# Attention over 512 queries per block of keys, with probabilities of four query tiles weighted together, in a hybrid attention and retention block on one Trainium2 core

## The chip, the cores and the metric

The program runs on one core of a Trainium2 chip. A core has a matrix engine, TensorE (PE in the profile; PEld is its weight load, which runs ahead of the matmuls), a VectorE (DVE), a ScalarE (ACT), a GpSimd (POOL) and a SyncE (SP), which here only issues transfers. Each engine has its own queue of instructions in program order, and they meet through semaphores. The metric is the device time of one execution in microseconds; the median of three runs is given.

## The reference

One layer over 2048 tokens of width 1024: an RMS norm, one input projection to ten pieces (7168 columns), two branches, a gated merge, an output projection and a last RMS norm. The branch that matters here is attention: 8 heads of width 64, in which a chunk of 64 frames attends to itself and the eight chunks before it, with a clipped relative bias.

```python
qc = qb.reshape(n_chunks, CHUNK, H, d)
k_band = jnp.concatenate([kp[i:i + n_chunks] for i in range(N_LEFT_CHUNKS + 1)], axis=1)
v_band = jnp.concatenate([vp[i:i + n_chunks] for i in range(N_LEFT_CHUNKS + 1)], axis=1)
s = jnp.einsum('nqhd,nkhd->nhqk', qc, k_band).astype(jnp.float32) * scale + bias[None]
s = jnp.where(valid[:, None, None, :], s, NEG_INF)
w = jax.nn.softmax(s, axis=-1).astype(vb.dtype)
o = jnp.einsum('nhqk,nkhd->nqhd', w, v_band)
```

The other branch is retention (8 heads, keys of 64, values of 128, in chunks), and each branch has its own output projection and gate.

## The kernel before

The large projections are **dense** work: a Strassen scheme over operands that are split into a high and a low float32r part, three matmuls of 128x512 per weight pair. It is one long generator, cut into steps; one step is three such matmuls on TensorE (some 0.7 us) with whatever their preparation and evacuation need elsewhere. Attention and retention run in two sequences, for the first 1024 tokens and then for the last, and between their own instructions they call `fill(n)`, which takes n steps of the dense generator. `later(n, fn)` puts work on a list that is issued n steps later, so the order of the instructions on every engine is written out by the step counter: TensorE, SyncE and (in these stages) all the other engines keep that program order (`Ordered`). In the attention stages the dense work is the gate projection (names ps_g, wh_g, wl_g, raw_g, t_g, u_g, c_g).

Queries come in blocks of 512 (b = 0..3), and a block in four tiles of 128 (t = 0..3). Before, a **unit** is a head, a block and a half (un): two query tiles, a = 0 and 1. For a unit `soft` (twice) multiplies the tile's queries by its 640 keys into the PSUM tile wide (four matmuls, 384 and 256 columns; less on block 0, which has no block before it). One step later VectorE adds the bias and takes the row minimum (`least`, the custom instruction pr<-wide,bt), one more step later ScalarE takes the exponentials with their sum (`exps`), and after four steps VectorE inverts the sum and GpSimd scales the row (`normed`, pr<-pr,rsum). Then `weighted` turns the probabilities (pr) with transposes into a PSUM tile tp, in three groups of two key tiles each, one group per step. ScalarE writes the high part (pth), one step later VectorE the low part (ptl<-tp,pth), and three steps after the transposes (PV_LAG) TensorE multiplies the values (va) by both parts into po. Each product is 128x256: key tile j times the two query tiles of the unit. A pair (key tile, query tile) that lies outside the band is a block of zeros in pth and ptl, set by a VectorE MEMSET. In the first and last group of a unit one of four blocks is such zeros. `out_` evacuates po after the second half.

A unit takes six steps (line 1585 on: soft, `fill(2 * ATT_FILL)`, soft, `fill(ATT_FILL)`, three groups with a fill each; one or two groups on block 0). 18 steps of dense work stand between the first loads of a stage and its first scores, 12 after its last group. Tiles of pools rotate: four pr tiles of 128x640 (PR_BUFS), and twelve 128x512 tiles of the pool E (E_ATT) for queries, values, pth, ptl, gates and results. ps_acc has four PSUM banks, for dense accumulators and tp both. Loads (qa queries, ka keys, va values, ua gates) are issued on SyncE's queue.

Of the kernel before, what the change touches and what calls it, by code (L numbers as in the profile page):

```python
# [21 lines left out]
P = 128  # L22
# [50 lines left out]
def hybrid_kernel(  # L73
# [30 lines left out]
    def r32(ap):  # L104
        return ap.bitcast(F32)
# [1306 lines left out]
    def attention(s, sbp, ps_wide):  # L1412
# [1 line left out]
        wide = ps_wide.tile([P, 1536], F32, tag="wide", name="wide")  # L1414
        po = ps_wide.tile([P, 512], F32, tag="po", name="po")
        kts, vts, qts, bts, uts, oas, prs = {}, {}, {}, {}, {}, {}, {}
        units = [(h, b, un) for h in range(HEADS) for b in (2 * s, 2 * s + 1) for un in range(2)]

        def load_k(h, b):
            kts[h, b] = sbp.tile([P, 2 * B], F32R, tag="kt", bufs=2, name=f"ka_{h}_{b}")  # L1420
# [52 lines left out]
            later(1, close)  # L1473
            later(0, far)

        def soft(h, b, un, a):

            t = 2 * un + a
# [18 lines left out]
            pr = sbp.tile([P, WIN], F32, tag="pr", bufs=PR_BUFS, name=f"pr_{nm}")  # L1497
            mn = small.tile([P, 1], F32, tag="mn", name=f"mn_{nm}")
            rsum = small.tile([P, 1], F32, tag="rsum", name=f"rsum_{nm}")
            bt = bts[h]  # L1500

            def least():
                dve.tensor_tensor_reduce(
                    pr[:, 0:w], sp, bt[:, WIN - w:WIN], 1.0, 3.0e38, ALU.add, ALU.min, mn,
                )

            def exps():
                act.activation(pr[:, 0:w], pr[:, 0:w], AF.Exp, bias=mn, scale=-1.0, accum_out=rsum)

            def normed():  # L1510
                dve.reciprocal(rsum, rsum)
# [5 lines left out]
            return pr  # L1517

        def weighted(h, b, un, pr2):

            nk = 6 if b > 0 else 2 * un + 2
            lo = [0, 1] if b > 0 else [0, 0]
            hi = [nk - 1, nk]
            o = po[:, un * 256:(un + 1) * 256]
            for gr in range(nk // 2):
                js = [2 * gr + 1, 2 * gr] if gr in (0, nk // 2 - 1) else [2 * gr, 2 * gr + 1]
                tp = ACC(f"tp_{h}_{b}_{un}_{gr}")
                ok, none, parts = [], [], []
                for n, j in enumerate(js):
                    for a in range(2):  # L1530
                        c = (2 * n + a) * P
                        if lo[a] <= j < hi[a]:
                            pe.transpose(
                                tp[:, c:c + P], pr2[a][:, (j - lo[a]) * P:(j - lo[a] + 1) * P], ident
                            )
                            ok.append(c)
                        else:
                            none.append(c)
                c0, c1 = ok[0], ok[-1] + P
                assert c1 - c0 == len(ok) * P  # L1540

                def part(which, gr=gr, tp=tp, none=none, parts=parts, c0=c0, c1=c1):
                    t = E(f"pt{which}_{h}_{b}_{un}_{gr}", F32R)
                    parts.append(t)
                    for c in none:
                        dve.memset(r32(t[:, c:c + P]), 0.0)
                    if which == "h":
                        act.copy(t[:, c0:c1], tp[:, c0:c1])
                    else:
                        dve.tensor_tensor(t[:, c0:c1], tp[:, c0:c1], r32(parts[0][:, c0:c1]), ALU.subtract)  # L1550

                def product(gr=gr, js=js, parts=parts):
                    for n, j in enumerate(js):
                        k = 2 * un + j if b > 0 else j + 4
                        v4 = vts[h, b - 1 + k // 4][:, k % 4, :]
                        for i, t in enumerate(parts):
                            pe.matmul(
                                o, v4, t[:, 256 * n:256 * n + 256],
                                start=(gr == 0 and n == 0 and i == 0),
                                stop=(gr == nk // 2 - 1 and n == 1 and i == 1),  # L1560
                            )
                    if gr == nk // 2 - 1:
                        later(1, out_)

                part("h")
                later(1, lambda part=part: part("l"))
                later(PV_LAG, product)
                yield

            def out_():  # L1570
                if un == 0:
                    return
# [4 lines left out]
                put(6, oascr[h // 2][b][64 * (h % 2):64 * (h % 2) + 64], oa)  # L1577

        load_bias(0)
        load_k(0, 2 * s)  # L1580
        load_q(0, 2 * s, 0)
        fill(12)
        turn_bias(0)
        fill(6)
        for m in range(len(units) + 1):
            if m < len(units):
                h, b, un = units[m]
                if m + 1 < len(units):
                    h2, b2, un2 = units[m + 1]
                    load_q(h2, b2, un2)  # L1590
                if un == 0 and m + 2 < len(units):
                    load_k(*units[m + 2][0:2])
                if un:
                    load_u(h, b)
                if (b, un) == (2 * s, 0) and h + 1 < HEADS:
                    load_bias(h + 1)
                if (b, un) == (2 * s + 1, 0) and h + 1 < HEADS:
                    turn_bias(h + 1)
                prs[m] = [soft(h, b, un, 0)]
                fill(2 * ATT_FILL)  # L1600
                prs[m].append(soft(h, b, un, 1))
                fill(ATT_FILL)
            if m:
                for _ in weighted(*units[m - 1], prs.pop(m - 1)):
                    fill(ATT_FILL)
            if m < len(units) and un == 0:
                later(PV_LAG - 1, lambda h=h, b=b: load_vs(h, b))
        fill(PV_LAG + 9)


    def retention(s, ps_ret):
# [427 lines left out]
```

## Time and profile before

| what | us |
|---|---|
| median of three runs (lowest, highest) | 1945.7 (1945.29, 1947.35) |
| the profiled execution: its time, its span | 1943.98, 1942.2 |
| TensorE matmul busy | 1887.3 (97%) |
| VectorE, ScalarE, GpSimd busy | 1355.7, 930.9, 898.4 |
| attention's score matmuls (wide), first and last start | 348.0 to 1321.7 |
| products with the values (po<-pth and po<-ptl), 336 each | 92.5 and 88.3 busy |
| VectorE MEMSET of pth and ptl, 112 each | 18.5 and 18.5 busy |

Attention stands at 348 to 562 us and at 1077 to 1335 us of the span, a retention stage behind each. Busy time of TensorE is a union of instructions whose ends are modelled, about 0.28 us for a 128x256 matmul; how fast they follow each other is read from the starts in the timeline. A row of a group reads: busy time, mean of one in ns, idle time before, and what ended it.

### The profile page before, as it was taken

The page shows a single profiled execution, that of the slowest core. Times are in us where ns is not written, and L with a number is a line of the kernel's source. Part 1 is how long each engine was busy: PE and PEld are TensorE (multiplying, and loading weights), DVE is VectorE, ACT ScalarE, POOL GpSimd, SP SyncE. Part 2 cuts the span into 40 slices and gives each one's busy share as a digit, 9 for nine tenths or more (in the row PEclk, how much of TensorE's full clock was granted, in tenths as well). Part 3 has the DMA queues.
Part 4 walks back from the last instruction along what each step waited for, and adds up shares of the span by engine and source line. Part 5 has one row for each costly group of instructions (what it writes and reads, how often), then busy time and mean ns, then how long its engine had stood idle before and what let it go on. Part 6 is the DMA issues. An engine that isn't in the chain of part 4 may idle for free. (4 is left out here: it accounts for less than half of the span.)

```text
span 1942.2 us, 31900 instructions
## 1 busy us (share of the span) xinstructions
PE 1887.3 (97%) x10437; PEld 1617.8 (83%) x10437; DVE 1355.7 (70%) x2521; ACT 930.9 (48%) x1931; POOL 898.4 (46%) x742
## 2 busy tenths in 40 slices
PE   7999999999999999999999999999999999999998
PEld 6899879888888887899879888888888878887886
DVE  6969788677756558879788677765555654547665
ACT  7544553666654545343333666664455321223554
POOL 0313525545545566323415544544564114557775
PEclk9999999999999999999999999999999999999999
DMA  6586876565559978575666555555998999977673
GB/s 195 169 279 194 255 263 217 182 192 177 175 156 277 270 239 298 186 257 187 196 222 209 158 166 174 160 155 160 272 274 269 313 357 330 320 261 237 208 240 127
DMA packets 325750, 435.93 MB, mean 224 GB/s; under 512 B 30073, under 2 KB 191377, under 8 KB 325585
## 3 DMA queue, kind: packets, MB, share of 16 engines
q1 hardware_dynamic: 260096, 368.35, 59.3%
q10 hardware_dynamic: 65488, 65.55, 11.2%
q8 instruction: 83, 1.36, 0.3%
q14 instruction: 83, 0.67, 0.1%
HBM read 288.14 MB, written 145.64 MB: 223 GB/s over the span
## 5 line engine op out<-in xcount | busy, mean ns | idle before, releaser
L142 POOL TENSOR_SCALAR pr<-pr,rsum 128x640 f32<-128x640 f32 (+4 forms) x128 | 96.5, 754 | 212.2 <-DVE ptl L142 99.8
L142 PE MATMUL ps_g_z<-r,wh_g 128*128 128x512 f32 x448 | 144.0, 403 | 1.4 <-DVE c_g L142 1.4
L142 PE MATMUL ps_g_x<-r,wh_g 128*128 128x512 f32 x448 | 143.2, 401 | 1.0 <-ACT u_g L142 0.8
L142 DVE CUSTOM_DVE_ANT_0 pr<-wide,bt 128x640 f32<-128x640 f32 (+4 forms) x128 | 94.3, 737 | 61.8 <-PE wide L142 49.7
L142 ACT ACTIVATE pr<-pr,mn 128x640 f32<-128x640 f32 (+4 forms) x128 | 98.0, 766 | 81.9 <-DVE mn L142 81.9
L142 DVE TENSOR_TENSOR ptl<-tp,pth 128x384 fp32r<-128x384 f32 x168 | 96.1, 573 | 41.2 <-ACT pth L142 37.9
L142 ACT CAST pth<-tp 128x384 fp32r<-128x384 f32 x168 | 84.5, 515 | 68.0 <-PE tp L142 64.8
L142 POOL TENSOR_TENSOR l_vr<-vrt,h_vr 128x512 fp32r<-128x512 f32 x32 | 46.8, 1463 | 121.0 <-DMA qrs<-l_q 81.3
L142 POOL TENSOR_TENSOR sl<-sm,sh 128x384 fp32r<-128x384 f32 x64 | 68.9, 1077 | 70.5 <-ACT sh L142 48.2
L142 PEld LDWEIGHTS tp<-ident,pr 128*128 128x128 f32 x560 | 71.1, 140 | 27.4 <-POOL pr L142 2.9
L142 DVE TENSOR_TENSOR sm<-sr,dm 128x384 f32<-128x384 f32 x64 | 35.6, 556 | 82.8 <-DMA dm<-in_dmask_dram 26.3
L142 POOL TENSOR_TENSOR wl_g<-t_g,wh_g 128x512 fp32r<-128x512 f32 x56 | 75.0, 1340 | 39.5 <-ACT wh_g L142 39.2
L142 PE MATMUL po<-pth,va 128*128 128x256 f32 x336 | 92.5, 296 | 0.0
L142 PE MATMUL tp<-ident,pr 128*128 128x128 f32 x560 | 89.3, 272 | 2.9 <-POOL pr L142 1.7
L142 ACT CAST wh_p<-raw_p 128x512 fp32r<-128x512 f32 x99 | 61.3, 621 | 61.7 <-PE ps_p_y L142 23.3
L142 PE MATMUL wide<-ka,qa 128*128 128x384 f32 (+1 forms) x448 | 88.3, 313 | 2.3 <-DVE mn L142 2.1
L142 PEld LDWEIGHTS wide<-ka,qa 128*128 128x128 f32 x448 | 74.5, 188 | 18.9 <-DVE mn L142 9.0
L142 PE MATMUL po<-ptl,va 128*128 128x256 f32 x336 | 88.3, 284 | 1.4
L142 PE MATMUL ps_g_z<-r,wl_g 128*128 128x512 f32 x224 | 88.3, 394 | 0.0
L142 PE MATMUL ps_g_x<-r,wl_g 128*128 128x512 f32 x224 | 88.1, 393 | 0.0
L142 DVE TENSOR_TENSOR wl_p<-raw_p,wh_p 128x512 fp32r<-128x512 f32 x99 | 82.4, 836 | 5.4 <-ACT wh_p L142 5.4
L142 POOL TENSOR_TENSOR t_g<-raw_g,t_g 128x512 f32<-128x512 f32 x56 | 73.7, 1316 | 24.6 <-DVE wl_g L142 10.6
(933 smaller groups left out, 6263.0 us busy)
## 6 DMA issues: line engine op xcount, KB each, us to landing
raw_g<-in_w_in_dram ACTq DMA_DIRECT2D x56, 512.0 KB, 4.3
raw_p<-in_w_in_dram ACTq DMA_DIRECT2D x38, 512.0 KB, 5.8
qa<-qas SPq DMA_DIRECT2D x128, 128.0 KB, 3.1
qr<-qrs SPq DMA_DIRECT2D x128, 128.0 KB, 4.6
vr<-vrs SPq DMA_DIRECT2D x64, 256.0 KB, 5.9
ka<-kas SPq DMA_DIRECT2D x56, 256.0 KB, 3.4
va<-vas SPq DMA_DIRECT2D x40, 256.0 KB, 3.3
kds<-kdt_k SPq DMA_DIRECT2D x32, 256.0 KB, 3.3
```

Source lines behind the costliest of these rows:

```text
L142: return tc.keep_in_program_order(op(*a, **k))
```

## The change

A unit is now a head and a block: all four query tiles, `weighted` with six groups of key tiles (0,1), 2, 3, 4, 5, (7,6), of which block 0 has the last three. A product takes key tile j with only those query tiles that see it: 1, 2, 3, 4, 4, 3, 2, 1 tiles for j = 0 to 7, that is 128 to 512 columns; the transposes put just these side by side, and the memsets of zero blocks are gone. On block 0 the four query tiles' probabilities (128, 256, 384 and 512 columns) share two pr tiles. There are five pr tiles for four, and eleven E tiles for twelve. A unit's steps are numbered: `plan` says at which of 12 steps (9 on block 0) each group of this unit and each `soft` of the next unit is issued, `slot` issues them, and one fill stands behind every slot. The first group's product comes four steps after its transposes, the others three. Ahead of a stage's first scores stand 12 + 2 steps and the slots of an empty unit, behind its last product 6. The number of dense steps in a stage is the same.

```diff
-E_ATT = 12
+E_ATT = 11
-PR_BUFS = 4
+PR_BUFS = 5
...
-        units = [(h, b, un) for h in range(HEADS) for b in (2 * s, 2 * s + 1) for un in range(2)]
+        units = [(h, b) for h in range(HEADS) for b in (2 * s, 2 * s + 1)]
...
-        def weighted(h, b, un, pr2):
-
-            nk = 6 if b > 0 else 2 * un + 2
...
-                    for c in none:
-                        dve.memset(r32(t[:, c:c + P]), 0.0)
...
-                            pe.matmul(
-                                o, v4, t[:, 256 * n:256 * n + 256],
...
+                pair, at = (t, 0) if b > 0 else ((0, 0), (1, 0), (1, 2 * P), (0, P))[t]
+                if (h, b, pair) not in wholes:
+                    wholes[h, b, pair] = sbp.tile([P, WIN], F32, tag="pr", bufs=PR_BUFS, name=f"pr_{nm}")
+                prs[h, b, t] = wholes[h, b, pair][:, at:at + w]
...
+        def weighted(h, b, gr):
+
+            k0 = 0 if b > 0 else 4
+            js = ((0, 1), (2,), (3,), (4,), (5,), (7, 6))[gr]
+            tp = ACC(f"tp_{h}_{b}_{gr}")
+            c, cut, parts = 0, [], []
+            for j in js:
+                ts = range(max(0, j - 4), min(4, j + 1))
+                cut.append((j, c, ts))
+                for t in ts:
+                    at = (j - max(t, k0)) * P
+                    pe.transpose(tp[:, c:c + P], prs[h, b, t][:, at:at + P], ident)
+                    c += P
...
+            def product():
+                for j, at, ts in cut:
+                    n = len(ts) * P
+                    v4 = vts[h, b - 1 + j // 4][:, j % 4, :]
+                    for i, p in enumerate(parts):
+                        pe.matmul(
+                            po[:, ts[0] * P:ts[0] * P + n], v4, p[:, at:at + n],
...
+            part("h")
+            later(1, lambda: part("l"))
+            later(PV_LAG + (gr == 0), product)
+
+        def plan(b):
+
+            if b == 0:
+                return 9, {2: 3, 4: 4, 6: 5}, {1: 0, 3: 1, 5: 2, 7: 3}
+            return 12, {0: 0, 2: 1, 4: 2, 6: 3, 8: 4, 10: 5},                 {2: 0, 6: 1, 8: 2, 10: 3} if s else {2: 0, 4: 3, 6: 1, 8: 2}
...
         load_bias(0)
-        load_k(0, 2 * s)
-        load_q(0, 2 * s, 0)
+        load_k(*units[0])
+        load_q(*units[0], 0)
         fill(12)
         turn_bias(0)
-        fill(6)
...
-        fill(PV_LAG + 9)
+        fill(2)
+        for m in range(-1, len(units)):
+            length, *plans = plan(units[m][1] if m >= 0 else 2 * s + 1)
+            for n in range(length):
+                slot(m, n, *plans)
+                if n == length - 2 and m + 2 < len(units):
+                    load_q(*units[m + 2], 0)
+                if n == length - 1 and m + 1 < len(units):
+                    load_vs(*units[m + 1])
+                fill(ATT_FILL if m >= 0 or n > 1 else 0)
+        fill(PV_LAG + 3)
```

Three places show how the instructions moved. In the names the head's number is left out, so pth_2_0 is block 2, group 0 (before: block 2, half 0, group 0 is pth_2_0_0). First TensorE in the second attention stage, block 2: the products of a first group before,

```order
L142 MATMUL po<-pth_2_0_0_13109,va_1_13082 128x256
L142 MATMUL po<-ptl_2_0_0_13116,va_1_13082 128x256
L142 MATMUL ps_g_1_z<-r_86,wh_g_1_4_12987 128x512
L142 MATMUL ps_g_1_z<-r_87,wh_g_1_4_12987 128x512
L142 MATMUL ps_g_1_z<-r_86,wl_g_1_4_12988 128x512
L142 MATMUL wide<-ka_3_13024,qa_3_0_13063 128x384
L142 MATMUL wide<-ka_3_13024,qa_3_0_13063 128x256
```

(the second of the two key tiles; the first has the same two rows just ahead) and now:

```order
L142 MATMUL po<-pth_2_0_13294,va_1_13275 128x128
L142 MATMUL po<-ptl_2_0_13306,va_1_13275 128x128
L142 MATMUL po<-pth_2_0_13294,va_1_13275 128x256
L142 MATMUL po<-ptl_2_0_13306,va_1_13275 128x256
L142 MATMUL ps_g_2_v<-r_90,wh_g_2_2_13109 128x512
L142 MATMUL ps_g_2_v<-r_91,wh_g_2_2_13109 128x512
L142 MATMUL ps_g_2_v<-r_90,wl_g_2_2_13110 128x512
L142 MATMUL tp_2_2_13352<-ident,pr_2_0_13139 128x128
L142 MATMUL tp_2_2_13352<-ident,pr_2_1_13204 128x128
L142 MATMUL tp_2_2_13352<-ident,pr_2_2_13233 128x128
L142 MATMUL tp_2_2_13352<-ident,pr_2_3_13270 128x128
```

The first key tile's products have lost their zero half, and between two groups' products there are now two dense steps or one with other work of the unit, where there was one. Second, VectorE at the same place, before,

```order
L142 MEMSET pth_2_0_0_13109 128x128
L142 TENSOR_TENSOR wl_g_1_6_13057<-raw_g_1_1_12734,wh_g_1_6_13056 128x512
L142 RECIPROCAL rsum_2_2_13074<-rsum_2_2_13074 128x1
L142 MEMSET ptl_2_0_0_13116 128x128
L142 TENSOR_TENSOR ptl_2_0_0_13116<-tp_2_0_0_13105,pth_2_0_0_13109 128x384
L142 TENSOR_TENSOR ptl_2_0_1_13133<-tp_2_0_1_13126,pth_2_0_1_13131 128x512
L142 MEMSET pth_2_0_2_13142 128x128
L142 RECIPROCAL rsum_2_3_13096<-rsum_2_3_13096 128x1
L142 MEMSET ptl_2_0_2_13151 128x128
L142 TENSOR_TENSOR ptl_2_0_2_13151<-tp_2_0_2_13138,pth_2_0_2_13142 128x384
```

and now:

```order
L142 TENSOR_TENSOR ptl_2_0_13306<-tp_2_0_13290,pth_2_0_13294 128x384
L142 RECIPROCAL rsum_2_3_13262<-rsum_2_3_13262 128x1
L142 TENSOR_TENSOR oa_3_13317<-po,oa_3_13317 64x512
L142 TENSOR_TENSOR ptl_2_1_13335<-tp_2_1_13322,pth_2_1_13326 128x384
L142 ISA pr_3_0_13337,mn_3_0_13332<-wide,bt_12794 128x640
L142 ISA mn_3_0_13332 128x1
L142 TENSOR_TENSOR u_g_2_13350<-ps_g_2_v,u_g_2_13153 128x512
L142 TENSOR_TENSOR wl_g_2_6_13309<-raw_g_2_1_12731,wh_g_2_6_13308 128x512
L142 TENSOR_TENSOR ptl_2_2_13363<-tp_2_2_13352,pth_2_2_13357 128x512
```

Three ptl followed each other with four memsets between them; now other work of the unit stands between two ptl. Third, GpSimd in the second stage, where before a tile's scaling (the fourth of a block, pr_2_3) stands behind two differences of the dense work,

```order
L142 TENSOR_SCALAR pr_2_2_13922<-pr_2_2_13922,rsum_2_2_13924 128x640
L142 TENSOR_TENSOR t_g_4_13978<-raw_g_4_0_13689 128x512
L142 TENSOR_TENSOR t_g_4_13980<-raw_g_4_1_13762,t_g_4_13978 128x512
L142 TENSOR_SCALAR pr_2_3_13949<-pr_2_3_13949,rsum_2_3_13951 128x640
L142 TENSOR_TENSOR oa_3_13953<-oa_3_13953,ua_3_13703 64x512
```

and such a place now:

```order
L142 TENSOR_TENSOR oa_2_15099<-oa_2_15099,ua_2_14969 64x512
L142 TENSOR_SCALAR pr_2_0_15119<-pr_2_0_15119,rsum_2_0_15115 128x640
L142 TENSOR_SCALAR pr_2_1_15181<-pr_2_1_15181,rsum_2_1_15176 128x640
L142 TENSOR_SCALAR pr_2_2_15210<-pr_2_2_15210,rsum_2_2_15204 128x640
L142 MEMSET bt_15072 64x64
L142 TENSOR_TENSOR t_g_7_15288<-raw_g_7_0_14817,raw_g_7_1_14892 128x512
L142 TENSOR_SCALAR pr_2_3_15244<-pr_2_3_15244,rsum_2_3_15236 128x640
```

The same instructions stand in the queue, in another grouping; dense differences stand between two scalings of a block as they did.

More of the change, by code (lines that the diff above doesn't have):

```diff
@@ new lines, in weighted, with part @@
+        def weighted(h, b, gr):
[10 more added lines that the diff above has]
+                    c += P
+            def part(which):
+                p = E(f"pt{which}_{h}_{b}_{gr}", F32R)
+                parts.append(p)
+                if which == "h":
+                    act.copy(p[:, 0:c], tp[:, 0:c])
+                else:
+                    dve.tensor_tensor(p[:, 0:c], tp[:, 0:c], r32(parts[0][:, 0:c]), ALU.subtract)
+            def product():
[5 more added lines that the diff above has]
+                            po[:, ts[0] * P:ts[0] * P + n], v4, p[:, at:at + n],
+                            start=j == (0 if b > 0 else 4) and i == 0, stop=gr == 5 and j == 6 and i == 1,
+                            skip_group_check=True,
+                        )
+                if gr == 5:
+                    later(1, out_)
@@ L1579, in attention @@
         load_bias(0)
-        load_k(0, 2 * s)
-        load_q(0, 2 * s, 0)
+        load_k(*units[0])
+        load_q(*units[0], 0)
         fill(12)
         turn_bias(0)
-        fill(6)
[L1585 to L1607, printed above, removed]
```

71 lines of the change are left out of this document (24 added, 47 removed).

## The prediction

> **What bounds the kernel now.** I read the page's busy times first, then the engines' busy time in two stretches from the middle of the attention stages, then the waits of the weight load there, then the timeline. In the windows the columns are length, then PE, PEld, DVE, ACT, POOL busy with instruction counts, clock, DMA share, GB/s.
>
> ```profile
> span 1942.2 us, 31900 instructions
> PE 1887.3 (97%) x10437; PEld 1617.8 (83%) x10437; DVE 1355.7 (70%) x2521; ACT 930.9 (48%) x1931; POOL 898.4 (46%) x742
> ...
> 362.00:550.00 188.00, 187.56 (x1093) 159.35 (x1093) 141.04 (x408) 121.21 (x282) 102.30 (x116) 1.00 0.61 181
> 1088.00:1322.00 234.00, 231.92 (x1395) 200.96 (x1394) 172.39 (x472) 143.10 (x311) 112.80 (x114) 1.00 0.55 166
> ```
>
> TensorE is full, at a granted clock of 1.00, and the next engine stands at about three quarters in the stages that the change touches (VectorE 141.0 of 188 and 172.4 of 234). But a busy share of TensorE hides short waits, since modelled ends overlap the next start. What its queue waited for shows at the weight load (us in total, times, longest), first stage, then second:
>
> ```profile
> PEld wide L142 <- DVE mn L142: 5.1, 14, 1.3
> PEld tp L142 <- POOL pr L142: 1.6, 3, 1.0
> PEld po L142 <- DVE ptl L142: 1.4, 5, 0.3
> ...
> PEld wide L142 <- DVE mn L142: 3.9, 6, 1.7
> PEld po L142 <- DVE ptl L142: 2.7, 9, 0.3
> PEld tp L142 <- DVE ptl L142: 2.0, 2, 1.0
> PEld tp L142 <- POOL pr L142: 1.3, 1, 1.3
> ```
>
> Together 18.0 us in some 470 us of attention. So the stages run at TensorE's pace: a column less is time won, and at most 18 us of waits can be won or moved.
>
> **The price of a matmul** is the distance between starts, not its duration. From the timeline of TensorE, inside the second attention stage and inside retention (start, us shown, what, count):
>
> ```profile
> 1148.42 0.62 PE L142 MATMUL ps_g_x<-r,wh_g 128*128 128x512 f32 x2
> 1148.88 0.40 PE L142 MATMUL ps_g_x<-r,wl_g 128*128 128x512 f32 x1
> 1149.12 0.74 PE L142 MATMUL wide<-ka,qa 128*128 128x384 f32 x4
> 1149.70 0.28 PE L142 MATMUL po<-pth,va 128*128 128x256 f32 x1
> 1149.82 0.28 PE L142 MATMUL po<-ptl,va 128*128 128x256 f32 x1
> ...
> 609.57 0.63 PE L142 MATMUL kv<-vr,kd 128*128 128x256 f32 x4
> ...
> 607.44 0.28 PE L142 MATMUL o<-sl,vr 128*128 128x128 f32 x1
> 607.55 0.27 PE L142 MATMUL o<-sh,vr 128*128 128x128 f32 x1
> 607.66 0.62 PE L142 MATMUL sr<-qr,kr 128*128 128x256 f32 x4
> ```
>
> Three of 512 columns take 1149.12 - 1148.42 = 0.70, so 0.233 each. One of 256 takes 0.12, and more finely, by the four kv, whose last is shown with 0.28 as the po are, (0.63 - 0.28)/3 = 0.117. The four wide (384, 256, 384, 256) take 0.58, so one of 384 takes (0.58 - 0.24)/2 = 0.17. One of 128, of the same float32r kind, takes 0.11: hardly less than one of 256. Below 256 columns something other than columns sets the pace; each of these matmuls loads its own weights.
>
> **Products: -8.0 us.** A block after the first had 24 products of 256 columns per head, 24 x 0.117 = 2.81. It now has four each of 128, 256, 384 and 512: 4 x (0.11 + 0.117 + 0.17 + 0.233) = 2.52. That is 0.29 less in each of 8 heads x 3 blocks, 6.9 us. On block 0, 12 products (1.40) become two of each size (1.26), 0.14 x 8 = 1.1. With 0.12 for 256 columns, as the single starts read, the two come to 9.8. I take 8.0, by the finer spacing. Transposes, scores and dense steps keep their count.
>
> **Waits for the low part: -4.0 us.** Here is one, TensorE, its weight load and VectorE:
>
> ```profile
> 1147.49 0.36 PE L142 MATMUL po<-pth,va 128*128 128x256 f32 x1
> 1147.97 0.39 PE L142 MATMUL po<-ptl,va 128*128 128x256 f32 x1
> ...
> 1147.96 0.19 PEld L142 LDWEIGHTS po<-ptl,va 128*128 128x128 f32 x1 [0.32 <-DVE ptl L142]
> ...
> 1146.70 0.66 DVE L142 TENSOR_TENSOR oa<-po,oa 64x512 f32<-64x512 f32 x1
> 1147.34 0.17 DVE L142 MEMSET ptl<- 128x128 f32 x1
> 1147.42 1.26 DVE L142 TENSOR_TENSOR ptl<-tp,pth 128x384 fp32r<-128x384 f32 x2
> ```
>
> The product stood 0.48 after its predecessor instead of 0.12: 0.36 lost, because VectorE came to ptl behind the evacuation of po and a memset. The waits above count 14 such, 14 x 0.36 = 5.0 us. Removed are all the memsets:
>
> ```profile
> L142 DVE MEMSET pth<- 128x128 f32 x112 | 18.5, 165 | 0.0
> L142 DVE MEMSET ptl<- 128x128 f32 x112 | 18.5, 165 | 0.0
> ```
>
> 37 us of VectorE, which is no time of the program by itself (VectorE is at 75% beside a full TensorE), but two of them, 0.33, stood before each such ptl. And ptl now comes every second step. Bounds 0 and -5.0; I take -4.0, since block 1's last group still has only dense steps between transposes and product.
>
> **Ends and starts of the stages: -4.7 us.** The long waits are single: 1.0 and 1.3 for GpSimd's pr at the last transposes of each stage, four steps after the last scores where seven lie in the middle, since no further unit stood between; now the last unit's groups have six steps or more like any other. I take 1.8 of the 2.3. The two of 1.0 of tp on ptl I read as a group that found the PSUM banks still held by earlier ones; one group in two steps gives them back sooner, 1.4 of 2.0. The longest of wide, 1.3 and 1.7, are the second queries' tile at each stage's start. Its load was issued three steps ahead; now it is six steps ahead in the second stage and two in the first, there before the store of the bias on SyncE's queue instead of behind it: 1.5 of 3.0. Together between 0 and -7.3, and -4.7 taken.
>
> **New waits: +3.5 us.** The scaled probabilities now have less cover. From a tile's scores to its first transpose lay seven steps for the later tile of a half; now six for three of the four tiles. GpSimd made 58 such in 234 us, 29 units of six steps, 8.07 us each, so a step is 1.34 us. What cover was left shows here, GpSimd's end against the transposes:
>
> ```profile
> 1140.72 0.81 POOL L142 TENSOR_SCALAR pr<-pr,rsum 128x640 f32<-128x640 f32 x1 [0.48 <-DVE ptl L142]
> 1145.08 0.49 PE L142 MATMUL tp<-ident,pr 128*128 128x128 f32 x3
> ...
> L142 POOL TENSOR_SCALAR pr<-pr,rsum 128x640 f32<-128x640 f32 x58 | 46.6, 804 | 118.5 <-DVE ptl L142 68.9 <-DVE rsum L142 46.3 <-ACT wh_g L142 3.3
> L142 POOL TENSOR_TENSOR wl_g<-t_g,wh_g 128x512 fp32r<-128x512 f32 x12 | 15.9, 1329 | 0.2
> L142 POOL TENSOR_TENSOR t_g<-raw_g,t_g 128x512 f32<-128x512 f32 x12 | 15.5, 1294 | 1.3 <-DVE wl_g L142 0.8
> L142 POOL TENSOR_TENSOR t_g<-raw_g 128x512 f32<-128x512 f32 x6 | 8.1, 1352 | 0.1
> ```
>
> 1145.08 - 1141.53 = 3.55 us were left, so about 2.2 remain. Two dense differences ahead of a scaling (1.35 + 1.29 = 2.65 us) can use that up where GpSimd gets them late. There are 6 such pairs in the window and 6 places with wl_g behind t_g (1.29 + 1.33); some 28 in both stages. Bounds: 0, if GpSimd is always through with them, and 28 x 1 us. GpSimd is idle half of the window (112.8 of 234), so I take 3.0, 0.1 each. Behind the stage, the first loads of retention wait on SyncE behind the last store of attention:
>
> ```profile
> 565.55 0.46 SPq L142 DMA_DIRECT2D oas<-oa  x1
> ...
> 566.75 1.30 SPq L142 DMA_DIRECT2D kr<-krs  x2
> 568.10 2.51 SPq L142 DMA_DIRECT2D qr<-qrs  x4
> ...
> 577.70 0.57 PE L142 MATMUL sr<-qr,kr 128*128 128x256 f32 x4
> ...
> qr<-qrs SPq DMA_DIRECT2D x128, 128.0 KB, 4.6
> ```
>
> That store now lies some five steps (3.5 us) nearer to retention's first scores. They need the loads of kr and two of qr, on the way by 569.4 and landed 4.6 later, at 574.0, 3.7 before the scores: the cover is nearly gone, not overdrawn. Bounds 0 and 2 x 2; I take 0.5.
>
> **The sum.** -8.0 - 4.0 - 4.7 + 3.0 + 0.5 = -13.2 us against the profiled execution's 1943.98 (span 1942.2, 1.8 around it): 1930.8. The median stands 1.7 above that execution: **1932.5**.
>
> **Rivals.** (a) Only the products' columns count: the waits stay in number, since every wait on VectorE comes back as one on GpSimd. 1945.7 - 8.0 = 1937.7. For it: the chain of the softmax lost a step. Against it: 37 us of VectorE are gone.
> (b) Columns set the price without a floor: then the sixth of the columns that goes is a sixth of the time, 24 x 0.47 + 8 x 0.23 = 13.1, and with the other terms 1927.4. Against it stands 0.11 for 128 columns, three starts of one kind. The Trainium skill, page "TensorE: Matmul & The Clock Gate", section "Back-to-back issue gap", has for a matmul by itself N/2.4 + 2.5 ns, 56 ns for 128 columns; by it the estimate of the saving would be some 12.5 us, near this rival. The trace has twice that for 128 columns, and the page says itself that a stream with weight loads is slower than its formula at small N.
> (c) Slower: GpSimd takes the wait's place. At each of the 28 places of two dense operations the scaling comes 2.65 + 0.8 us after them, and the next one after that; if TensorE loses a full 1 us at each, that is +28 in place of +3.0, and 1932.5 + 25 = 1957.5; it decides from 0.6 us a place, where 28 x 0.6 = 17 are all that the other terms win (16.2). For it: the second order listing of GpSimd. Against it: GpSimd's idle half.
> (d) It doesn't shorten the stage: what TensorE saves is given back because the four-tile chain sets the pace (each unit's po is free for the next only after evacuation, with one or two steps between). 1945.7. Against it: 470 us of attention with 18 us of waits.
>
> **Chances.** Forecast 0.57, (a) 0.20, (b) 0.07, (c) 0.06, (d) 0.10. Faster by over 0.2% (3.9 us, about what a measurement of this kernel can tell from no change) holds the forecast, (a) and (b): 0.84; no change 0.10; slower 0.06. The range is 1924 (products by columns, 13.1, and the 8.7 of waits with no new ones: 1945.7 - 21.8) to 1943 (products, no wait won, and 5 us of new ones).
>
> **What would show it.** Right: po<-pth of four sizes in the groups, start distances of 0.11, 0.12, 0.17, 0.23; no MEMSET of pth; the waits of po on ptl under 1 us in sum; no wait of 1 us at tp or wide at the ends of the stages; attention's two stages together about 12 us shorter and every other stage as long as before. Wrong: tp waiting for POOL pr many times over; sr waiting for qr at the start of retention; 128-column products spaced 0.06; or the stages shorter but what follows longer.

## The result, and the profile after

| | before | changed |
|---|---|---|
| median (lowest to highest) of seven runs each, us | 1945.29 (1942.84 to 1947.35) | 1933.78 (1929.67 to 1938.71) |
| ratio, 95% interval | | 0.9948 (0.9931 to 0.9964) |
| the profiled execution: time, span | 1943.98, 1942.2 | 1932.45, 1930.7 |

The changed kernel is 0.5% faster: 11.5 us by the medians, with 13.2 us forecast. From the head of the changed kernel's page:

```profile
PE 1876.8 (97%) x10213; PEld 1606.8 (83%) x10213; DVE 1335.1 (69%) x2297; ACT 931.1 (48%) x1931; POOL 899.0 (47%) x742
```

The 224 memsets are gone (2521 instructions of VectorE became 2297), and the 672 products are now 448 (10437 matmuls became 10213). TensorE's share did not move, as the time fell with its work.

**Where the time went.** I cut the span at four marks that both kernels have: the first matmul of each gate projection, with which an attention stage begins, and the first score matmul of the retention stage behind it. Timeline of TensorE, before, then changed (the mark at 577.70 stands in the prediction):

```profile
321.63 0.63 PE L142 MATMUL ps_g_x<-r,wh_g 128*128 128x512 f32 x2
...
1046.51 0.63 PE L142 MATMUL ps_g_x<-r,wh_g 128*128 128x512 f32 x2
...
1350.37 0.57 PE L142 MATMUL sr<-qr,kr 128*128 128x256 f32 x4
```

```profile
320.90 0.63 PE L142 MATMUL ps_g_x<-r,wh_g 128*128 128x512 f32 x2
...
573.22 0.57 PE L142 MATMUL sr<-qr,kr 128*128 128x256 f32 x4
...
1043.20 0.63 PE L142 MATMUL ps_g_x<-r,wh_g 128*128 128x512 f32 x2
...
1339.43 0.57 PE L142 MATMUL sr<-qr,kr 128*128 128x256 f32 x4
```

| stretch, us | before | changed | difference |
|---|---|---|---|
| start to first gate matmul | 321.63 | 320.90 | -0.7 |
| first attention stage | 256.07 | 252.32 | -3.8 |
| between | 468.81 | 469.98 | +1.2 |
| second attention stage | 303.86 | 296.23 | -7.6 |
| from the second retention scores to the end | 591.83 | 591.27 | -0.6 |

The two stages that the change touches won 11.4 us; all the rest together moved by 0.1. That the rest agrees so closely is chance: with the same code in it, the stretch between the stages took from 465.6 to 477.0 us in the runs below. The attention stages are the better ruler. The total of one kernel scatters by some 9 us (1929.67 to 1938.71 above), but the second attention stage, in four executions in which TensorE has the same work in the same order there, took 296.23, 296.40, 296.19 and 296.43 us. The first stage is looser: 252.2 to 253.4 with the same order. Of the kernel before there is one profiled execution.

**The products' pace.** TensorE in the second stage of the changed kernel: 128 and 256 columns behind dense work, then 512, then 384, both behind scores:

```profile
1190.48 0.22 PE L142 MATMUL po<-pth,va 128*128 128x128 f32 x1
1190.54 0.27 PE L142 MATMUL po<-ptl,va 128*128 128x128 f32 x1
1190.65 0.33 PE L142 MATMUL po<-pth,va 128*128 128x256 f32 x1
1190.82 0.28 PE L142 MATMUL po<-ptl,va 128*128 128x256 f32 x1
1190.94 0.63 PE L142 MATMUL ps_g_z<-r,wh_g 128*128 128x512 f32 x2
...
1163.16 0.39 PE L142 MATMUL po<-pth,va 128*128 128x512 f32 x1
1163.39 0.39 PE L142 MATMUL po<-ptl,va 128*128 128x512 f32 x1
...
1168.71 0.34 PE L142 MATMUL po<-pth,va 128*128 128x384 f32 x1
1168.89 0.34 PE L142 MATMUL po<-ptl,va 128*128 128x384 f32 x1
1169.06 0.63 PE L142 MATMUL ps_g_x<-r,wh_g 128*128 128x512 f32 x2
```

The first distance reads 0.06, which the prediction had named as a sign that it was wrong. But the next ones read 0.11, 0.17 and 0.12: I read it as a start that is recorded early for the second product, and the third's distance is the longer for it. The four together take 0.46, where four of 256 took 0.47 before (0.117 each). A single distance misleads here; the sum over a group does not. Two of 384 take 0.35, and one of 512 takes 0.23. So a later block has 2 x 0.46 for the groups (0,1) and (7,6), 2 x 0.46 for the two of 512 and 2 x 0.35 for the two of 384: 2.54 against 24 x 0.117 = 2.81. 0.27 x 24, and 1.40 - 1.27 = 0.13 on block 0 of each of 8 heads, make 7.5 us.

**The waits.** What the weight load waited for in the two attention stages of the changed kernel (us in total, times, longest), first stage, then second:

```profile
PEld wide L142 <- DVE mn L142: 4.3, 8, 1.5
PEld tp L142 <- POOL pr L142: 1.0, 3, 0.4
PEld po L142 <- DVE ptl L142: 0.8, 2, 0.4
PEld po L142 <- DVE oa L142: 0.5, 1, 0.5
PEld po L142 <- ACT pth L142: 0.4, 2, 0.2
...
PEld po L142 <- DVE oa L142: 6.0, 10, 0.9
PEld wide L142 <- DVE mn L142: 1.1, 2, 0.9
PEld po L142 <- DVE ptl L142: 0.5, 2, 0.3
```

By these rows the waits for ptl fell from 4.1 to 1.3 us, those of tp from 4.9 to 1.0, those of wide from 9.0 to 5.4. A new one of 6.5 us stands against them: the first product of a unit waits until VectorE has read po of the unit before (oa). In sum 18.0 became 14.6. One of the new waits, in lines chosen from the timelines of the engines:

```profile
1234.87 0.69 ACT L142 COPY bt<-bt 128x128 f32<-128x128 f32 x3
1235.46 0.63 ACT L142 ACTIVATE g<-u_g 128x512 f32<-128x512 f32 x1
1235.93 0.80 POOL L142 TENSOR_SCALAR pr<-pr,rsum 128x640 f32<-128x640 f32 x1 [0.51 <-DVE rsum L142]
1236.00 0.61 ACT L142 CAST wh_g<-raw_g 128x512 fp32r<-128x512 f32 x1
1236.12 1.14 DVE L142 SCALAR_TENSOR_TENSOR g<-g,u_g 128x512 f32<-128x512 f32 x1 [0.39 <-ACT g L142]
1236.63 0.59 ACT L142 COPY oa<-po 64x512 f32<-64x512 f32 x1
1237.17 0.40 PE L142 MATMUL ps_g_z<-r,wl_g 128*128 128x512 f32 x1
1237.24 0.68 DVE L142 TENSOR_TENSOR oa<-po,oa 64x512 f32<-64x512 f32 x1
1237.98 0.19 PEld L142 LDWEIGHTS po<-pth,va 128*128 128x128 f32 x1 [0.85 <-DVE oa L142]
```

There is one po for all units. ScalarE copies one half of it, VectorE adds the other half to the copy, and only then may TensorE overwrite it. The addition stands behind a dense sum, but it could not start before the copy ended either (1236.63 + 0.59 = 1237.22). And the copy starts where ScalarE's dense cast ends, in a run of work without a gap. So it is in the whole second stage: at 9 of the 10 waits the addition starts within 0.04 us of the copy's end (at the tenth 0.20), and every one of the copies starts 0.02 to 0.03 behind a cast of wh_g. So although the wait is put down to VectorE, what comes late is ScalarE's copy; no run moved the cast out of its way. The product starts with its weight load, 0.81 after the dense matmul ahead of it in place of 0.23.

### The profile page after: what moved, and what is told of

It reads as the page before. It is cut to its first block, busy times and chain, and to the rows that moved or that the text cites. A ratio compares the mean times of both kernels' runs of the same rounds, so it can differ in the third digit from the quotient of the medians.

```text
span 1930.7 us, 31188 instructions
## 1 busy us (share of the span) xinstructions
PE 1876.8 (97%) x10213; PEld 1606.8 (83%) x10213; DVE 1335.1 (69%) x2297; ACT 931.1 (48%) x1931; POOL 899.0 (47%) x742
## 5 line engine op out<-in xcount | busy, mean ns | idle before, releaser
L142 POOL TENSOR_SCALAR pr<-pr,rsum 128x640 f32<-128x640 f32 (+4 forms) x128 | 100.5, 786 | 196.4 <-DVE rsum L142 129.5
L142 DVE TENSOR_TENSOR ptl<-tp,pth 128x512 fp32r<-128x512 f32 (+1 forms) x168 | 100.2, 597 | 91.8 <-ACT pth L142 77.5
L142 ACT CAST pth<-tp 128x512 fp32r<-128x512 f32 (+1 forms) x168 | 85.2, 507 | 39.1 <-PE tp L142 34.4
L142 PE MATMUL wide<-ka,qa 128*128 128x384 f32 (+1 forms) x448 | 95.0, 328 | 2.2 <-DVE mn L142 2.0
L142 PEld LDWEIGHTS ps_g_z<-r,wh_g 128*128 128x128 f32 x448 | 80.0, 190 | 15.0 <-issue 2.4
L142 PEld LDWEIGHTS ps_g_x<-r,wh_g 128*128 128x128 f32 x448 | 79.4, 188 | 13.9 <-ACT u_g L142 2.2
L142 DVE TENSOR_TENSOR wl_p<-t_p,wh_p 128x512 fp32r<-128x512 f32 x80 | 65.3, 817 | 23.6 <-ACT wh_p L142 23.6
```

The source lines that it names most:

```text
L142: return tc.keep_in_program_order(op(*a, **k))
```

## The experiments

Each gives the median with its ratio to the kernel before, in runs shared within a job (kernel before: 1943.46, then 1944.56, then 1944.52 us in the three jobs), and the two attention stages, cut as above.

| kernel | median, us | ratio (95%) | first stage | second stage |
|---|---|---|---|---|
| before | 1945.29 | | 256.07 | 303.86 |
| changed | 1933.78 | 0.9948 (0.9931 to 0.9964) | 252.32 | 296.23 |
| changed, again | 1933.45 | 0.9944 (0.9929 to 0.9959) | 252.22 | 296.40 |
| products padded to pairs | 1939.8 | 0.9982 (0.9972 to 0.9992) | 255.18 | 300.49 |
| memsets put back | 1933.53 | 0.9948 (0.9932 to 0.9964) | 253.33 | 298.20 |
| without the products of 128 | 1925.21 | 0.991 (0.9895 to 0.9925) | 250.00 | 291.34 |
| before, without the zeros | 1939.1 | 0.9977 (0.9964 to 0.9989) | 255.76 | 301.58 |
| first product a step later | 1932.96 | 0.9937 (0.9918 to 0.9955) | 254.45 | 292.81 |
| queries loaded earlier | 1936.39 | 0.9954 (0.9937 to 0.9970) | 252.35 | 296.19 |
| four dense steps to the tail | 1931.41 | 0.9935 (0.9913 to 0.9957) | 254.27 | 296.22 |
| state loaded first | 1932.84 | 0.9933 (0.9918 to 0.9948) | 252.39 | 296.43 |
| later in the second stage, state first | 1931.4 | 0.9926 (0.9907 to 0.9945) | 253.39 | 292.85 |
| the same, four steps to the tail | 1930.29 | 0.9922 (0.9906 to 0.9938) | 254.39 | 292.89 |

**The order of the steps alone: products padded back to pairs of 256 columns.**

```diff
+                for pair in ((0, 1), (2, 3)):
+                    if not set(pair) & set(ts):
+                        continue
+                    cut.append((j, c, pair))
...
+                for z in none:
+                    dve.memset(r32(p[:, z:z + P]), 0.0)
```

> The changed kernel's order of steps, but every product again on two query tiles (256 columns, 24 per block after the first), with the zero blocks and their 224 memsets as before. Theory (products cost by their starts, 0.113 at 128 to 0.232 at 512; memsets hardly matter once ptl is spaced): the changed kernel's time + 7.6 us of TensorE, + 0 to 2 for memsets, so 1941 to 1944. Rival (columns without a floor): + 13, so 1947. Rival (the new order of steps does most of the gain): about 1935 to 1937.

1939.8 us lies between the theory's range and that of the last rival. The stages are 2.9 and 4.3 us longer than the changed kernel's, 7.1 in sum, near the theory's 7.6, and 4.3 us in sum shorter than before's. So narrow products with the memsets gone bring 7.1 of the 11.4 us, and the new order with its other buffers the remaining 4.3. What the two parts of the 7.1 are worth alone, this run doesn't tell.

**The memsets alone, put back into the changed kernel** (224, of 128 columns each, into the unused part of pth and ptl).

```diff
+                if c < 512:
+                    dve.memset(r32(p[:, c:512]), 0.0)
```

> The changed kernel with the 224 memsets of 128x128 put back on VectorE where they stood, into columns that nothing reads; products as changed. Theory (a group in two steps leaves VectorE time): within 2 us of the changed kernel, and waits of po on ptl under 1.5 us in sum. Rival (memsets were what made ptl late): + 4 us, and the waits of po on ptl back at 4 to 5 us. Either way the wait of the first group's product for the evacuation of po grows by up to 0.3 us in each of 16 units, 0 to 5 us.

The total does not show them (1933.53 us). The stages do: 1.0 us in the first, where the same code can differ by as much, and 2.0 in the second, where it repeated to 0.2. Of the waits of the weight load, one row of the first and one of the second stage:

```profile
PEld po L142 <- DVE ptl L142: 1.3, 5, 0.4
...
PEld po L142 <- DVE oa L142: 8.3, 12, 1.1
```

In the new order the waits for ptl come to 1.8 us in both stages, little above the changed kernel's 1.3 and over the 1.5 that the theory allowed; the waits for oa grow, 8.3 us for 6.0. How the memsets do it isn't shown: in the second stage at 10 of the 12 waits the addition still came behind ScalarE's copy, and at two behind a memset. So by the stages the memsets cost 2 to 3 us here. If they cost as much beside padded products, the narrow products alone would be worth some 4 to 5 of the 7.1 us above; no run has padded products without memsets.

**The price of 128 columns: those products left out.** This kernel leaves out the part of attention that the first and last key tile of each unit contribute.

```diff
                     n = len(ts) * P
+                    if n == P:
+                        continue
...
-                            start=j == (0 if b > 0 else 4) and i == 0, stop=gr == 5 and j == 6 and i == 1,
+                            start=j == (1 if b > 0 else 4) and i == 0, stop=gr == 5 and j == 6 and i == 1,
```

> The changed kernel without its 112 products of 128 columns (the first and last key tile's part of attention is left out, nothing else). Theory (a floor of 0.113 us below 256 columns): 112 x 0.113 = 12.7 us less. Rival (time by columns, 0.058 each): 6.5 us less. If units wait for the evacuation of po anyway, up to 3 us of either is given back.

TensorE at the same place as above, and the waits of the first and second stage:

```profile
1187.50 0.28 PE L142 MATMUL po<-pth,va 128*128 128x256 f32 x1
1187.62 0.28 PE L142 MATMUL po<-ptl,va 128*128 128x256 f32 x1
1187.73 0.62 PE L142 MATMUL ps_g_z<-r,wh_g 128*128 128x512 f32 x2
```

```profile
PEld wide L142 <- DVE mn L142: 5.5, 13, 1.6
...
PEld po L142 <- DVE oa L142: 8.7, 13, 1.0
```

The group takes 0.23 without them and 0.46 with them (0.238 and 0.460 by the medians of 41 such groups behind dense work in each kernel): 0.22 for two, 0.11 each. That gives the price by the starts. The time alone would not have told it: 56 pairs x 0.22 = 12.4 us of TensorE's work went, but the stages became only 2.3 + 4.9 = 7.2 us shorter, near the rival's 6.5. The waits of wide and po rose; some 5 us came back as waits, more than the 3 that were allowed for. That the evacuation of po takes as long as before, so that TensorE with less work ahead meets it sooner, is how I read it.

**Memsets and zero halves taken from the kernel before,** in its old order.

```diff
-                    for c in none:
-                        dve.memset(r32(t[:, c:c + P]), 0.0)
...
-                                o, v4, t[:, 256 * n:256 * n + 256],
+                                o[:, z0:z1], v4, t[:, 256 * n + z0:256 * n + z1],
```

> The kernel before, with its own order of steps and units, where the zero blocks are not written and not multiplied: 224 memsets gone, 224 products of 256 columns are 128 columns now. Theory (floor; memsets only part of why ptl is late): products -0.9 us (224 x 0.004), waits of po on ptl fall by 1 to 3 of 5 us, so 1.5 to 4 us under the kernel before. Rival (columns without a floor): 224 x 0.058 = -13 us. Rival (memsets are the cause of the late ptl): -5 us with no wait of po on ptl left.

4.4 us by the shared runs (1943.46 - 1939.1, interval 2 to 7), 2.6 in the two stages, most in the second; the latter is inside the theory's range. The waits in the first stage, then the second:

```profile
PEld po L142 <- DVE ptl L142: 1.0, 5, 0.3
...
PEld wide L142 <- DVE mn L142: 3.6, 6, 1.7
...
PEld tp L142 <- POOL pr L142: 1.4, 1, 1.4
PEld po L142 <- DVE ptl L142: 0.2, 1, 0.2
```

Without the memsets the waits for ptl fall from 4.1 to 1.2 us in the old order too. The spacing brings them down with the memsets in place (1.8 us in the run with the memsets put back), and the lack of memsets does in the old order: each is enough for most of them. The long waits of tp and wide at the ends and starts stay, so what the changed kernel won there belongs to its order.

**The new wait, moved: a unit's first product one step later.**

```diff
-            later(PV_LAG + (gr == 0), product)
+            later(PV_LAG + 2 * (gr == 0), product)
```

> The changed kernel with the first product of a unit's first group placed one step later. Theory (the new wait in front of a unit's first product is VectorE still reading po of the unit before, 6.0 us in 10 waits in the second attention stage, some 3.3 us of TensorE's time, and place decides it): those waits fall below 1.5 us, the stage from the first score matmul after the first projection to the second retention score is 1 to 3 us shorter, about 1931 to 1932 us in all. Rival (VectorE is simply full there, and the wait moves to the next scores, wide waiting for mn): the po waits go but wide's waits rise by as much, and the time stays at 1933 to 1935 us.

The longest waits of the second stage, then that of the first:

```profile
PEld tp L142 <- POOL pr L142: 1.4, 2, 0.9
PEld wide L142 <- DVE mn L142: 1.2, 3, 0.9
...
PEld wide L142 <- DVE mn L142: 7.1, 12, 1.5
```

In the second stage the wait for oa is gone and the stage is 3.4 us shorter (292.81; 292.85 and 292.89 in the last two kernels, which have the same). So its 6.0 us at the weight load were worth 3.4 us, and in that stage the place of the product decides; the rival's longer waits of wide did not come there (1.2 us, as before). In the first stage, where the wait was only 0.5 us, the stage is 2.1 us longer with the same edit, of which about 1 is within its scatter, and wide waits 7.1 us where it waited 4.3. By the stages 1.3 us remain; the total, 0.8 us lower by the medians, cannot tell that from nothing.

**One step earlier** was tried as well.

```diff
-            later(PV_LAG + (gr == 0), product)
+            later(PV_LAG, product)
```

> The changed kernel with the first product of a unit's first group one step earlier. Theory (place decides): each of the 28 units meets the evacuation of po some 0.5 us or more before it is done; with 0.3 to 0.6 us a unit it is 8 to 15 us slower, 1941 to 1949 us, and the waits of po for VectorE's oa grow in both attention stages. Rival (VectorE's fullness decides, not the place): within 2 us of the changed kernel, 1932 to 1936 us.

It came to 1935.49 us (ratio 0.9951, 0.9932 to 0.9971), with stages of 256.2 and 296.6, near the rival. It decides nothing: at this place the product stands ahead of the addition in program order, so it overwrites po before that half is read, and what is computed is no longer this attention; the wait that was to be lengthened is partly removed.

**The wait at a stage's start: both query loads issued ahead of the leading steps.**

```diff
+                if m >= 0:
+                    load_q(h, b, 1)
...
+        load_q(*units[0], 1)
         fill(12)
```

> The changed kernel with both loads of queries of a stage's first unit issued ahead of the leading twelve steps of projections. Theory (the first score matmul of each stage waits for the second load, 1.26 us at 349 and 0.62 us at 1075): both waits below 0.2 us, about 1.5 to 1.9 us faster, 1931.9 to 1932.3. Rival (the wait is for something else there, such as the first keys, or the evacuations of the projections are merely late by as much): waits of the same size stay under another name, 1933 to 1934 us.

The rival holds in its mechanism: the stages are unchanged, and so is the wait, though the loads were issued some 7 us earlier. The total, 1936.39 us, is above either range, with nothing in the stages to account for it. VectorE, GpSimd and the weight load at the start of the first stage of the changed kernel:

```profile
346.75 1.29 POOL L142 TENSOR_TENSOR t_g<-raw_g 128x512 f32<-128x512 f32 x1
346.94 1.65 DVE L142 TENSOR_TENSOR wl_g<-t_g,wh_g 128x512 fp32r<-128x512 f32 x1
348.51 0.68 DVE L142 CUSTOM_DVE_ANT_0 pr<-wide,bt 128x512 f32<-128x512 f32 x1
349.25 0.30 PEld L142 LDWEIGHTS wide<-ka,qa 128*128 128x128 f32 x2 [1.55 <-DVE mn L142]
```

and in the run with early loads:

```profile
348.42 0.30 PEld L142 LDWEIGHTS wide<-ka,qa 128*128 128x128 f32 x2 [1.54 <-DVE mn L142]
```

The scores wait for wide to be read, and VectorE reads it late because a dense subtraction stands ahead of it, which here takes 1.65 us. The queries' transfer has no part in it.

**Four leading dense steps moved behind the last unit.**

```diff
-        fill(12)
+        fill(8)
...
-        fill(PV_LAG + 3)
+        fill(PV_LAG + 7)
```

> The changed kernel with four of the twelve leading steps of projections moved behind the last attention unit of each stage (the count of steps is unchanged). Theory (the retention unit that follows starts too early for its loads and state, since attention ends sooner: the wait of o for the state's copy is 1.89 us at 1349 where it was 0.42): this wait falls below 0.6 us, 1.5 to 2 us faster, up to 4 with the first stage, 1930 to 1932 us. Rival (the retention unit's start is bound by its own chain from scores to state, not by when its loads were issued): the wait stays at 1.5 us or more, 1933 to 1935 us; with eight leading steps the first scores might also start ahead of their queries, which would show as wide waiting 2 us or more for a DMA.

The scores at the start of the first stage no longer wait, but the stage is 2.0 us longer: other dense work now meets the units, and the waits of wide are 4.9 us, those of po for oa 2.3. At retention's start o still waits 1.8 us at the weight load where it was 2.2. The first rival holds for that wait; the sign of the second, wide waiting for a DMA, is not there. The lower median (1931.41) has no place in the two stages; its interval holds the changed kernel's ratio.

**The retention state loaded first,** with the changed kernel run again beside it.

```diff
-        load_scored(*todo[1])
         load_state(*todo[0])
+        load_scored(*todo[1])
```

> The changed kernel itself once more, beside the variants of the same job, so that they can be told from it and not only from the kernel before. 1932 to 1935 us; the waits of po for VectorE's oa in the second attention stage again 6 us, the first matmul of o in the second retention stage again 1.5 to 2 us late.

Both came as expected: the waits for oa 6.1 us in the second stage, o 1.8 us.

> The changed kernel with the loads of the retention state issued ahead of the second set of keys and queries at the start of the second retention stage. Theory (o waits there because SyncE's queue comes to the state's load only at 1344.9, behind loads that wait for buffers): the wait of 1.9 us at o is gone, the state is landed before it is needed, and the stretch from the first retention score to the end of that stage is about 2 us shorter; 1931.5 to 1932.5 us in all. Rival (the queue as a whole is late, and one load's gain is another's loss): the wait turns up again as kv waiting for its values vr or as scores waiting for queries, 1 us or more, and the time stays at 1933 to 1935 us.

The timeline of the changed kernel at the start of the second retention stage, SyncE's queue, VectorE and the weight load:

```profile
1344.93 1.70 SPq L142 DMA_DIRECT2D state<-sts  x1
1348.46 0.48 DVE L142 SCALAR_TENSOR_TENSOR state<-state,kv 64x128 f32<-64x128 f32 x2 [3.10 <-DMA state<-sts]
1349.13 0.30 PEld L142 LDWEIGHTS o<-qr,sstk 128*128 128x128 f32 x2 [2.21 <-issue]
```

and the waits there with the state first:

```profile
PEld kv L142 <- ACT sh L142: 1.8, 1, 1.8
PEld kv L142 <- DMA vr<-vrs: 1.2, 2, 1.0
```

With the state's load at 1341.38 o no longer waits. But kv, which waited 0.8 us in the changed kernel of the same job, waits 3.0. From the first retention score of that stage to its last it took 156.9 us, and 156.4 in the changed kernel of the same job. So the rival's account fits: the queue of loads as a whole is late, and one load's gain is another's loss. The edit isn't even needed for the exchange: in the run with the early queries, which has the changed kernel's code from there on, o waits 0.2 us and kv 1.8 for vr.

**The later product in the second stage alone, with the state first, and then with the tail too.**

```diff
-            later(PV_LAG + (gr == 0), product)
+            later(PV_LAG + (1 + s) * (gr == 0), product)
```

> The changed kernel with the state's loads first, and with a unit's first product one step later in the second attention stage alone. Theory (in the second stage po's evacuation was the wait, worth 3.4 us from the first score after the projections to retention; in the first stage the later product gave 2 us back as waits of wide): second attention stage 3 to 3.5 us shorter, first stage as in the changed kernel, some 5 us in all with the state, 1928 to 1930 us. Rival (what the first stage lost when the product came later was chance of that run, and so may be the gain): 1931 to 1934 us.

> As the run with the state's loads first and the later product in the second stage, and four of the twelve leading dense steps moved behind the last unit of each stage. Theory (the wait of 1.2 us at the start of the first stage was VectorE, at a 1.65 us dense subtraction ahead of the scores' minimum; with other dense steps there it was 0.07): 1 to 2 us less than without that move, 1927 to 1929 us. Rival (the wait only moves, since the same dense work comes elsewhere): no less than without it, 1928 to 1931 us.

1931.4 and 1930.29 us, beside 1933.45 for the changed kernel in the same job; both lie in the rivals' ranges. In the second stage both win 3.4 to 3.5 us, as expected. The first stands 1.1 us higher in the one, whose order there is the changed kernel's, and 2.1 higher in the other, as with the tail alone. So the stages account for 2.3 us of the first kernel's gain and 1.3 of the second's. Their intervals (0.9907 to 0.9945, 0.9906 to 0.9938) overlap the changed kernel's, so they beat the kernel before clearly and the changed kernel probably, by the part that the second stage shows; what 1930.29 has beyond that is not explained.

## Why the prediction was right, point by point

- **Products, -8.0:** right as TensorE's work, 7.5 by the groups' pace. As time it is shown only together with the memsets: padding the products back with them cost 7.1, and putting the memsets back alone cost 2 to 3. So the sum's other reading, that 37 us of VectorE are no time of the program by themselves, failed in the new order, and how much of the 7.1 is the products' stays open. The floor of 0.11 for 128 columns is shown by leaving them out, and rival (b) falls with it, by the starts. By the formula of the Trainium skill, page "TensorE: Matmul & The Clock Gate", section "Back-to-back issue gap", a group of two of 128 and two of 256 would take 0.33 us; it took 0.46.
- **Waits of po for the low part, -4.0:** right in size at the weight load (4.1 to 1.3) but too large in time. The forecast's sign, under 1 us left, was missed by a little. By the starts in the kernel before, 12 of the 14 waits lost 0.34 to 0.39 and two 0.05, 4.4 us in all and not 5.0. Taking the memsets away in the old order, which brought these waits to 1.2, won 2.6 us in the stages, some of it by narrower products. And the two causes named, memsets and spacing, are not two shares: either change alone brings most of the waits down.
- **Ends and starts of the stages, -4.7:** the ends went as forecast, the waits of tp for pr and ptl from 4.9 to 1.0. The starts failed: "the second queries' tile" was not what wide waited for. Its longest wait came to 1.55 us in the first stage against 1.3, and 0.89 in the second against 1.7, and neither moved when the queries were loaded earlier; the rows that the prediction shows name VectorE's mn for both. What fell instead is the number of waits of wide, 20 to 10.
- **New waits, +3.0 of tp for GpSimd's pr:** the place was wrong. They came to 1.0 us in 3 places, less than before, and rival (c) with them to nothing. The new wait came where the prediction had put rival (d): po, one for all units, free only after its evacuation, at 11 of the 30 places where a unit follows another, 6.5 us at the weight load in sum, of which the second stage's 6.0 were worth 3.4 us of time. It doesn't undo the gain, as (d) would have had it, but it is what the sum lacked. That it is nearly the size of what was put on GpSimd is luck, and the total came out close partly for that reason.
- **Retention's first loads, +0.5:** of the kind that was forecast, late loads, but not the loads named: sr waits for no more than before, and o waits 2.2 us at the second stage (0.9 before), behind the state's load. In another run of the same code there it was 0.2, so it is no fixed cost, and what it costs cannot be told: from its first to its last score that stage took 156.0 us before, 157.7 in the changed kernel, and 156.4 in the changed kernel again.
- **The sum:** -13.2 forecast, -11.5 measured, of which 11.4 in the two stages. If the products' 7.5 were all won, 3.9 would be left for all waits, where 5.2 net were forecast; the padded kernel gives 4.3 for the new order. Rival (a), products only at 1937.7 us, falls with the 4.3 us that the new order brings without any narrower product.

## What to carry to other kernels

Where one engine is full, work taken from it is not all won as time: 12.4 us less of products gave 7.2, since what it waits for (here, as the rows read, one accumulator's evacuation on two other engines) does not get faster. Ask for each buffer that exists once which instructions lie between its last use and its next, and place the next user behind them by one step rather than beside them; how far is a matter of each stage, as the same step won 3.4 us in one and lost some 1 to 2 in the other. Look behind the engine that a wait is put down to: VectorE was named, and ScalarE's queue was what it waited for. And measure a change of a few us in the stretches of the trace that it touches, where the same code repeated to 0.2 us in one stage and 1.2 in the other, rather than in totals that scatter by 9.

## What the runs showed of the hardware

VectorE's dense subtraction wl_g<-t_g,wh_g, with two operands in SBUF, takes 0.68 us by the median of its 56 executions and up to 1.67. The groups of one tile's instructions in the changed kernel (duration in ns: lowest, median, highest):

```profile
L142 DVE TENSOR_TENSOR wl_g<-t_g,wh_g x56: 674/682/1670, 319.9 to 1471.6; 128x512 fp32r<-128x512 f32 x56
```

In the row at 346.94 it ends at 348.59, 0.55 after GpSimd's t_g of 346.75 ends (348.04). In the run with early query loads both stand 0.83 earlier (GpSimd 345.92 for 1.29, VectorE 346.11 for 1.64), and the end is again 0.54 behind GpSimd's; so it is with g<-g,u_g at 1236.12, which ends 0.53 after GpSimd's pr. These rows read as VectorE standing still until GpSimd is through. The Trainium skill, page "SBUF — State Buffer", section "Who interferes with whom", has this as a rule: a VectorE instruction with two SBUF inputs and a GpSimd instruction that reads SBUF exclude each other, and the later one waits; the traces agree. No run here took the overlap away by itself, so its share of the waits is not measured: it stands ahead of the wait at the first stage's start and of 3 of the 10 waits for oa in the second stage (g taking 1.24, 1.21 and 1.14 us there). At two of these three ScalarE's copy ended only 0.03 and 0.04 us ahead of the addition, and at the other 7 VectorE stood idle until that copy was done, so for the waits for oa it can matter little.
